# A hybrid encoder on one core: dense matmuls placed between transposes, score products and norm sums, with TensorE's order pinned to the source

## Chip, cores and metric

The kernel runs on one core of one Trainium2 chip. The metric is the device time of one execution in microseconds; lower is better. Five engines run side by side, each through its own list of instructions: TensorE (PE; its weight loads are shown apart as PEld), VectorE (DVE), ScalarE (ACT), GpSimd (POOL) and SyncE (SP, which issues DMAs). An engine whose next instruction waits for another engine stands still, and so does everything behind it in its list.

## What is computed

Two layers of an encoder over 512 tokens of 1024 features, in float32. Each layer mixes tokens in three ways from one projection of the normed input, merges the three by gates, and goes on with a gated feed-forward part and a small embedding part. Cut to what matters here:

```python
for i in range(DEPTH):                                   # DEPTH = 2
    h = rmsnorm(x, mix_norm[i])
    u_rnn, u_gelu, c_q, ckv_rope, fq, fk, fv, f_logit, gate_logit = split_columns(h @ w_in[i])
    y_a = rglru_branch(u_rnn, u_gelu, ...) @ w_br_a[i]   # gated recurrence
    y_b = mla_branch(c_q, ckv_rope, ...) @ w_br_b[i]     # latent attention, 8 heads
    y_c = fox_branch(fq, fk, fv, f_logit, ...) @ w_br_c[i]   # forgetting attention, 8 heads
    g = sigmoid(gate_logit + gate_b[i]).reshape(B, S, 3, D)
    x = x + (g[:, :, 0] * y_a + g[:, :, 1] * y_b + g[:, :, 2] * y_c) @ w_o[i]
    hf = rmsnorm(x, ffn_norm[i]) @ w_gate_up[i]
    x = x + (silu(hf[..., :D_FF]) * hf[..., D_FF:]) @ w_down[i]
    x = x + sigmoid(rmsnorm(x, ple_norm[i]) @ w_ple_gate[i]) * (p[i] @ w_ple[i])
return rmsnorm(x, final_norm)

# both attentions, per head and block of 128 queries (fox adds decay[t] - decay[s] to the logits)
s = where(mask, einsum('bqhd,bkhd->bhqk', q_blk, k) * scale, NEG_INF)
o = einsum('bhqk,bkhd->bqhd', softmax(s), v)
```

## The kernel before

**Products.** Every float32 operand is held as two float32r parts, hi and lo, whose sum is the value. A product of a 128x128 weight tile with 128 features of all 512 tokens is then three matmuls, hi by hi, hi by lo and lo by hi (`mm3`, L239), all into one PSUM bank. There are eight banks, of which the program's names `bank_67` to `bank_74` speak. `dense` (L246) is a generator for one output tile: it takes a bank, runs `mm3` once per k tile (8 for 1024 features), yields after each k tile, and hands the bank to its evacuation on VectorE or ScalarE. `group` and `values` are the same for several output tiles side by side; `values` makes the attention's values, token-major.

**Weights.** `Stream` keeps them flowing: SyncE loads units of four tiles, ScalarE casts the hi part (L112), VectorE subtracts to get the lo part (L113). A ring holds five split units. This work stands in the lists of ScalarE and VectorE among all the rest.

**Norms.** `norm_sum` sums squares over the partitions with four matmuls of one column (operand `one`), takes 1/sqrt with a dozen tiny VectorE instructions, and builds diagonals of it, hi and lo, with four instructions each. `norm_bcast` spreads them over all partitions with two matmuls (operand `onesr`). `after_norm` (L352) runs the first dense products behind a norm and puts sums and broadcast between their steps.

**Attention.** `attention(fox, odd, plan, tail)` is one loop over steps t, eight heads by four query tiles and three steps more. Step t does, in the source: the score products of tile t (two matmuls for fox, three for the latent attention, 128 to 512 columns wide); the products with the values of a head whose four tiles are done (`pv_mm`, eight matmuls); the transposes of tile t-2 (one to four, 128x128, L828, operand `identr`); on VectorE the mask addition (`fmask`, fox only, L221), the row maximum (L836) and, for tile t-1, the reciprocal and the scaling by it (L842, L225); on ScalarE the exponential (L230); and the copies of the transposed tile as `pth` (ScalarE, L853) and `ptl` (VectorE, L221). The values' products read `pth` and `ptl`. At the end of a step `fill` runs a share of the dense products that `plan` lists for this pair of heads: what is left, divided by the steps left, in k tiles. The plan holds merges, gates, branch projections, the projections of the next heads, and in fox's last pair the norm sums and broadcasts of the two latent norms.

**What sets the order.** Within the source's data dependences the framework's scheduler reorders each engine's instructions by a simulated timeline (`schedule_with_timeline_sim=True`). An instruction given to `tc.keep_in_program_order` keeps its place among others so given. Before, none of TensorE's instructions in attention is. Each engine then runs its list in order.

Of the kernel before, what the change touches and what calls it, by code (L numbers as in the profile page):

```python
# [17 lines left out]
DEPTH, SEQ, D = 2, 512, 1024  # L18
# [8 lines left out]
# columns of w_in  # L27
# [3 lines left out]
# columns of the small per-partition vectors, per layer  # L31
V_MIX, V_FFN, V_PLE, V_GB, V_CW, V_CB, V_BA, V_BX, V_QN, V_KN, V_BF = (
    0, 8, 16, 24, 48, 64, 68, 72, 76, 79, 81)
NV = 82
V_LAM = DEPTH * NV          # lambdas of all layers, side by side
# [3 lines left out]
NUNITS = 606                # units of four 128x128 weight tiles in the stream  # L39
KEPT = NUNITS - 16          # from here on the stream is kept on chip: it is used twice  # L40
PACKED = (8, 9, 311, 312)  # units whose tiles hold the parts of 64 columns side by side


class Pages:
    """Pages of one tile, handed out oldest-freed first."""
# [39 lines left out]
class Stream:  # L85
    """The weights, in the order in which TensorE uses them: loaded ahead, split into two
    float32r parts that sum to the float32 value."""
# [46 lines left out]
    def tile(self, spec):  # L134
        """hi and lo of the next 128x128 tile"""
# [7 lines left out]
    def again(self, i):  # L143
        """tile i of the stream, one of those that were kept"""
        return self._parts(i // 4, slice(128 * (i % 4), 128 * (i % 4) + 128))
# [6 lines left out]
    def wide(self, spec):  # L152
        """hi and lo of a 128x512 tile, at the start of a unit"""
# [13 lines left out]
class Trunk:  # L167
    def __init__(self, ctx, tc, wst, vec, xT, pT, trig, masks, outT, last):
# [32 lines left out]
        self.defer = None  # L201

    # -- small things ---------------------------------------------------------------------

    def cols(self, n):
        """n columns of a ring of small per-partition values"""
# [29 lines left out]
    def mm(self, out, a, b, start, stop):  # L236
        self.nc.tensor.matmul(out, a, b, start=start, stop=stop, skip_group_check=True)  # L237

    def mm3(self, out, ah, al, bh, bl, start, stop):  # L239
        self.mm(out, ah, bh, start, False)  # L240
        self.mm(out, ah, bl, False, False)
        self.mm(out, al, bh, False, stop)

    # -- products, as generators that stop after every k tile -----------------------------

    def dense(self, spec, xs, evac, m=128):  # L246
        """out[m, tokens] = sum over k of W[k, m] * X[k, tokens]; xs are pages"""
        b = self.banks.take()
        n = len(xs)
        for k, x in enumerate(xs):  # L250
            wh, wl = self.w.tile(spec + (k,))
            self.mm3(b[:m], wh[:, :m], wl[:, :m], x.h, x.l, k == 0, k == n - 1)
# [6 lines left out]
    def group(self, specs, xs, evacs):  # L259
        """several of them side by side, k tile by k tile"""  # L260
        bs = [self.banks.take() for _ in specs]
        n = len(xs)
        for k, x in enumerate(xs):
            for b, spec in zip(bs, specs):
                wh, wl = self.w.tile(spec + (k,))
                self.mm3(b[:, :], wh, wl, x.h, x.l, k == 0, k == n - 1)
# [1123 lines left out]
```

## Time and profile before

| what | value |
|---|---|
| runs of the kernel, median of 3 | 1825.26 us |
| lowest and highest | 1824.38, 1826.84 us |
| the profiled execution, from first to last instruction (its span) | 1825.0 us |
| mean granted clock of TensorE | 0.996 of full speed |
| ScalarE's casts of the weights (L112) | 590, 364.3 us busy |
| VectorE's subtractions for the weights (L113) | 590, 404.2 us busy |
| score and value products (L237 from `pr`) | 704, 120.7 us busy |

The profile gives no time of that execution beside its span; the span lies 0.26 us below the median of the runs. A row of a timeline reads: start, length, engine, line, operation, output and input by the program's names with buffer numbers left out, their shapes, and a count where like instructions follow each other. In brackets stands the idle time ahead of it with the instruction that ended it. An instruction's length includes its way through the engine's pipeline, so that the next one starts before it ends. A row of windows has the length of the stretch, each engine's busy time with its count of instructions, TensorE's granted clock, the busy share of the DMA engines and their GB/s.

### The profile page before, as it was taken

Reading aid. Unit: us, or ns where it says so; the run is one execution under the profiler, and the core shown is the slowest. Engines: PE = TensorE matmul, PEld = TensorE weight load, DVE = VectorE, ACT = ScalarE, POOL = GpSimd, SP = SyncE. Lnnn points to the kernel's source line nnn. Section 1 sums busy time; section 2 is a strip of 40 time slices with the busy share of each in tenths; the row PEclk is TensorE's granted clock in tenths of the full one; section 3 lists DMA queues with packets and bytes.
Section 4 is the critical chain, followed back from the end, with each engine's and each line's share of the span. In section 5 each row is a group of like instructions: output and inputs, shape, how many; then the busy total and the mean of one; then the engine's idle time right before and its main releaser. Section 6 shows DMA issues by size and latency. Waiting matters only on the chain. (4 is left out here: it accounts for less than half of the span.)

```text
span 1825.0 us, 24155 instructions
## 1 busy us (share of the span) xinstructions
PE 1807.5 (99%) x8490; PEld 1505.6 (82%) x8490; DVE 1210.6 (66%) x2421; ACT 817.1 (45%) x1562; POOL 117.2 (6%) x234
## 2 busy tenths in 40 slices
PE   9999999999999999999999999999999999999998
PEld 8778888888888888888887788888888888888887
DVE  8997678866665555444778966888576555553457
ACT  4766556553333333223447655565533333332243
POOL 1220001100000000000103200010000000000000
PEclk9999999999999999999999999999999999999999
DMA  5232223324222222322333322242232222232231
GB/s 178 91 131 82 81 78 117 97 72 139 96 95 96 96 98 98 110 94 97 133 110 122 106 81 82 91 116 85 87 128 92 99 98 97 95 109 99 98 116 47
DMA packets 98826, 184.17 MB, mean 101 GB/s; under 512 B 13552, under 2 KB 14752, under 8 KB 98704
## 3 DMA queue, kind: packets, MB, share of 16 engines
q1 hardware_dynamic: 89280, 162.04, 25.7%
q0 software_dynamic: 8416, 19.45, 3.8%
q8 instruction: 66, 1.08, 0.2%
q10 hardware_dynamic: 1008, 1.14, 0.2%
q14 instruction: 56, 0.46, 0.1%
HBM read 173.98 MB, written 4.21 MB: 98 GB/s over the span
## 5 line engine op out<-in xcount | busy, mean ns | idle before, releaser
L237 PE MATMUL bank<-pr,hl 128*128 128x512 f32 (+1 forms) x6812 | 1602.9, 392 | 2.8 <-ACT pr L233 1.1
L237 PEld LDWEIGHTS bank<-pr,hl 128*128 128x128 f32 (+1 forms) x6812 | 1269.9, 188 | 267.3 <-ACT pr L233 2.0
L112 ACT CAST hl<-raw 128x512 fp32r<-128x512 f32 x590 | 364.3, 618 | 672.0 <-PE bank L237 403.8
L113 DVE TENSOR_TENSOR hl<-raw,hl 128x512 fp32r<-128x512 f32 x590 | 404.2, 686 | 378.6 <-ACT hl L112 360.4
L221 DVE TENSOR_TENSOR pf<-pf 128x512 f32<-128x512 f32 (+3 forms) x235 | 151.1, 651 | 31.8 <-ACT pf L230 29.9
L221 DVE TENSOR_TENSOR pf<-bank,pf 128x512 f32<-128x512 f32 (+3 forms) x198 | 132.8, 676 | 58.6 <-PE bank L237 32.1
L230 ACT ACTIVATE pf<-pf 128x512 f32<-128x512 f32 (+1 forms) x145 | 86.1, 600 | 112.7 <-DVE pf L221 110.5
L237 PE MATMUL bank<-pr 128*128 128x256 f32 (+5 forms) x704 | 120.7, 303 | 4.1 <-ACT pf L230 2.2
L237 PEld LDWEIGHTS bank<-pr 128*128 128x128 f32 (+1 forms) x704 | 102.7, 191 | 14.1 <-ACT pf L230 2.7
L221 DVE TENSOR_TENSOR pr<-pf,pr 128x512 fp32r<-128x512 f32 (+2 forms) x126 | 85.6, 682 | 4.5 <-ACT pr L233 3.5
L230 ACT ACTIVATE pf<-bank,small 128x384 f32<-128x384 f32 (+3 forms) x130 | 68.9, 531 | 38.5 <-DVE small L836 35.4
L233 ACT CAST pr<-pf 128x512 fp32r<-128x512 f32 (+1 forms) x114 | 70.4, 620 | 33.2 <-DVE pf L218 23.1
L853 ACT CAST pth<-bank 128x128 fp32r<-128x128 f32 (+3 forms) x128 | 54.0, 427 | 58.7 <-PE bank L828 50.5
L221 DVE TENSOR_TENSOR ptl<-bank,pth 128x128 fp32r<-128x128 f32 (+3 forms) x128 | 61.7, 485 | 13.9 <-ACT pth L853 9.9
L836 DVE TENSOR_REDUCE small<-bank 128x1 f32<-128x384 f32 (+3 forms) x128 | 61.6, 484 | 7.6 <-PE bank L237 6.5
L237 PE MATMUL bank<-hl,pr 128*128 128x512 f32 x240 | 56.3, 391 | 0.4 <-DVE hl L113 0.4
L828 PE MATMUL bank<-identr,pf 128*128 128x128 f32 x320 | 55.0, 273 | 0.0
L237 PEld LDWEIGHTS bank<-hl,pr 128*128 128x128 f32 x240 | 44.7, 188 | 10.3 <-DVE hl L113 1.1
L225 DVE TENSOR_SCALAR pf<-pf,small 128x384 f32<-128x384 f32 (+3 forms) x128 | 48.6, 383 | 2.6
L828 PEld LDWEIGHTS bank<-identr,pf 128*128 128x128 f32 x320 | 40.2, 140 | 8.3
L218 DVE SCALAR_TENSOR_TENSOR pf<-pf,bank 128x512 f32<-128x512 f32 x48 | 32.6, 683 | 21.6 <-PE bank L237 21.2
L230 ACT ACTIVATE pf<-bank,vec 128x512 f32<-128x512 f32 x60 | 40.9, 689 | 12.9 <-PE bank L237 12.5
(112 smaller groups left out, 796.6 us busy)
## 6 DMA issues: line engine op xcount, KB each, us to landing
raw<-wst SPq DMA_DIRECT2D x606, 256.0 KB, 2.6
pf<-xT POOLq DMA_DIRECT2D x16, 256.0 KB, 3.3
pr<-pr POOLq DMA_DIRECT2D x32, 128.0 KB, 2.6
pf<-xs POOLq DMA_DIRECT2D x16, 256.0 KB, 3.2
pf<-trig POOLq DMA_DIRECT2D x12, 256.0 KB, 3.1
pf<-xT SPq DMA_DIRECT2D x8, 256.0 KB, 5.3
xs<-pf POOLq DMA_DIRECT2D x8, 256.0 KB, 2.7
pf<-pT POOLq DMA_DIRECT2D x4, 256.0 KB, 3.1
```

The costliest lines, as they stand in the source:

```text
L112: self.nc.scalar.copy(hi, src)
L113: self.nc.vector.tensor_tensor(lo, src, hi.bitcast(F32), op=ALU.subtract)
L218: self.nc.vector.scalar_tensor_tensor(out, a, s, b, op0=op0, op1=op1)
L221: self.nc.vector.tensor_tensor(out, a, b, op=op)
L225: self.nc.vector.tensor_scalar(out, a, s1, None, op0=op0)
L230: return self.nc.scalar.activation(out, a, f, **kw)
L233: self.nc.scalar.copy(hi, src)
L237: self.nc.tensor.matmul(out, a, b, start=start, stop=stop, skip_group_check=True)
L828: nc.tensor.transpose(T[:, c], p2.ap[:, c], self.ident[:, :])
L836: nc.vector.reduce_max(R[t][:, 0:1], S[:, :m], axis=AX.X, negate=True)
L853: self.nc.scalar.copy(hi, src)
```

## The change

`fill` now counts single matmuls, not k tiles. It puts one dense matmul ahead of every transpose and between the score products of a tile; what is left of a step's share comes at its end. `mm3` became a generator, `mm3s`, that yields between its three matmuls, and `dense`, `group` and `values` yield with it. While `attention` runs, `self.pinned` is set, and every matmul and transpose is given to `keep_in_program_order`, so that TensorE runs them as the source has them. `norm_sum` can run one matmul of the dense products between its four, and `after_norm` makes use of that. The tail of the last steps is 14 matmuls instead of 6 k tiles. Comments went too, and lines moved by a few: L237, L218, L221 and L225 are L238, L219, L222 and L226 after, the transposes L828 are L849, L836 and L842 are L857 and L863.

```diff
     def mm(self, out, a, b, start, stop):
-        self.nc.tensor.matmul(out, a, b, start=start, stop=stop, skip_group_check=True)
+        i = self.nc.tensor.matmul(out, a, b, start=start, stop=stop, skip_group_check=True)
+        if self.pinned:
+            self.tc.keep_in_program_order(i)
 
     def mm3(self, out, ah, al, bh, bl, start, stop):
+        self.run(self.mm3s(out, ah, al, bh, bl, start, stop))
+
+    def mm3s(self, out, ah, al, bh, bl, start, stop):
         self.mm(out, ah, bh, start, False)
+        yield
         self.mm(out, ah, bl, False, False)
+        yield
         self.mm(out, al, bh, False, stop)
...
     def dense(self, spec, xs, evac, m=128):
...
-            self.mm3(b[:m], wh[:, :m], wl[:, :m], x.h, x.l, k == 0, k == n - 1)
+            yield from self.mm3s(b[:m], wh[:, :m], wl[:, :m], x.h, x.l, k == 0, k == n - 1)
             yield
...
-    def norm_sum(self, st, n, fold=None):
+    def norm_sum(self, st, n, fold=None, between=None):
...
             self.mm(b[:, j:j + 1], acc.ap[:, j * 128:(j + 1) * 128], self.one[:, 0:1], True, True)
+            if between is not None:
+                between()
...
         for i, _ in enumerate(gen):
-            if i + 1 == s1:
-                self.norm_sum(st, n)
-            if i + 1 == s2:
+            if i + 1 == 3 * s1:
+                self.norm_sum(st, n, between=lambda: next(gen))
+            if i + 1 == 3 * s2 - st["n"] // 128:
                 self.norm_bcast(st)
...
-            def fill(m):
-                nonlocal left
+            def fill(m=1):
+                nonlocal left, spent
+                if t >= n and not todo:
+                    next(tail, None)
                 while m > 0 and todo:
                     try:
                         next(todo[0])
                         m -= 1
                         left -= 1
+                        spent += 1
                     except StopIteration:
                         todo.pop(0)
...
+            self.pinned = True
             for t in range(n + 3):
...
-                    left = sum(c for _, c in plan[t // 8])
+                    left = 3 * sum(c for _, c in plan[t // 8])
+                share, spent = -(-left // (8 - t % 8)), 0
...
                         self.mm(S[:, :m], q.h[:, c], k.h[:, :m], True, False)
+                        fill()
                         self.mm(S[:, :m], q.l[:68, c], k.l[:68, :m], False, True)
...
-                        nc.tensor.transpose(T[:, c], p2.ap[:, c], self.ident[:, :])
+                        fill()
+                        self.tc.keep_in_program_order(
+                            nc.tensor.transpose(T[:, c], p2.ap[:, c], self.ident[:, :]))
...
-                    fill(-(-left // (8 - t % 8)))
+                    fill(share - spent)
                 else:
                     drain()
-                    for _ in range(6):
+                    for _ in range(14):
                         next(tail, None)
...
+            self.pinned = False
```

The lists of instructions show what this moves. **TensorE, start of layer 0's fox attention**, right behind the last matmuls of the values. Before, where rows with `pr,hl` are dense matmuls and rows with `pr` alone are score products:

```order
L237 MATMUL bank_68<-pr,hl 128x512 x9
L237 MATMUL bank_73<-pr 128x128
L237 MATMUL bank_68<-pr,hl 128x512 x5
L237 MATMUL bank_69<-pr 128x256
L237 MATMUL bank_70<-pr,hl 128x512
L237 MATMUL bank_68<-pr,hl 128x512 x10
L237 MATMUL bank_70<-pr,hl 128x512 x5
L237 MATMUL bank_73<-pr 128x128
L237 MATMUL bank_69<-pr 128x256
```

The same place after the change. The piece begins with the second score product of tile 0; ahead of it, behind the values, stand only that tile's first product and one dense matmul:

```order
L238 MATMUL bank_73<-pr 128x128
L238 MATMUL bank_68<-pr,hl 128x512 x19
L238 MATMUL bank_69<-pr 128x256
L238 MATMUL bank_68<-pr,hl 128x512
L238 MATMUL bank_69<-pr 128x256
L238 MATMUL bank_68<-pr,hl 128x512 x3
L238 MATMUL bank_70<-pr,hl 128x512 x16
L238 MATMUL bank_71<-pr 128x384
L238 MATMUL bank_70<-pr,hl 128x512
L238 MATMUL bank_71<-pr 128x384
L238 MATMUL bank_70<-pr,hl 128x512
L849 MATMUL bank_74<-identr,pf 128x128
```

The second score product stood 30 dense matmuls behind the values and stands one behind them now; the first transpose (L828, now L849) stood 126 dense matmuls behind the values and stands 42 behind them now. In layer 1 it is 132 before and 42 after.

**VectorE in the same stage.** Its list is the same before and after up to the fourth evacuation of the values and one scalar_tensor_tensor (`pf<-pf,vec`) behind it. From there before has 35 instructions up to and with the scaling of tile 0, the last row of this piece:

```order
L113 TENSOR_TENSOR hl<-raw,hl 128x512
L221 TENSOR_TENSOR pr<-pf,pr 128x512
L842 RECIPROCAL small<-small 128x1
L836 TENSOR_REDUCE small<-bank_68 128x1
L221 TENSOR_TENSOR pr<-pf,pr 128x512
L221 TENSOR_TENSOR bank_73<-bank_73,fmask 128x128
L225 TENSOR_SCALAR pf<-pf,small 128x128
```

After the change there are 23, the last of which are:

```order
L857 TENSOR_REDUCE small<-bank_69 128x1
L222 TENSOR_TENSOR pr<-pf,pr 64x512
L219 SCALAR_TENSOR_TENSOR pf<-pf,vec 128x512
L222 TENSOR_TENSOR pr<-pf,pr 64x512
L219 SCALAR_TENSOR_TENSOR pf<-pf,vec 128x512
L863 RECIPROCAL small<-small 128x1
L857 TENSOR_REDUCE small<-bank_71 128x1
L863 RECIPROCAL small<-small 128x1
L222 TENSOR_TENSOR pr<-pf,pr 128x512
L226 TENSOR_SCALAR pf<-pf,small 128x128
```

The scaling of tile 0 moved forward by twelve instructions. In layer 1 there are 43 instructions of VectorE from the low part of head 0's queries to that scaling.

**TensorE from the latent norms' sums to their broadcasts**, in fox's last pair of heads, layer 0. The sums are the rows with `one`, the broadcasts those with `onesr`. Before:

```order
L237 MATMUL bank_69<-one,pf 128x1 x4
L237 MATMUL bank_70<-pr,hl 128x512 x18
L237 MATMUL bank_68<-pr 128x256 x2
L828 MATMUL bank_74<-identr,pf 128x128 x4
L237 MATMUL bank_70<-pr,hl 128x512 x6
L237 MATMUL bank_72<-pr,hl 128x512 x7
L237 MATMUL bank_67<-pr,onesr 128x512
L237 MATMUL bank_72<-pr,hl 128x512 x5
L237 MATMUL bank_73<-pr 128x384 x2
L237 MATMUL bank_72<-pr,hl 128x512
L237 MATMUL bank_69<-pth,pr 128x512
L237 MATMUL bank_67<-pr,onesr 128x512
```

After, from the second of the two score products behind the sums (fifteen dense matmuls, a score product and one dense matmul stand between the sums and this piece):

```order
L238 MATMUL bank_70<-pr 128x256
L238 MATMUL bank_69<-pr,hl 128x512
L849 MATMUL bank_68<-identr,pf 128x128
L238 MATMUL bank_69<-pr,hl 128x512
L849 MATMUL bank_68<-identr,pf 128x128
L238 MATMUL bank_69<-pr,hl 128x512
L849 MATMUL bank_68<-identr,pf 128x128
L238 MATMUL bank_69<-pr,hl 128x512
L849 MATMUL bank_68<-identr,pf 128x128
L238 MATMUL bank_69<-pr,hl 128x512 x4
L238 MATMUL bank_67<-pr,onesr 128x512 x2
L238 MATMUL bank_73<-pr,onesr 128x512 x2
```

The four transposes stand one by one between dense matmuls, and the four broadcasts follow each other behind 24 dense matmuls, where before they lay scattered behind 31 and more. In the latent attention six dense matmuls (three for the first head) and three score products of 384 columns now stand between the four transposes of a head's last tile and its products with the values. Of the norms outside attention, the sums are separated in the two embedding norms; elsewhere they stay in a row, since the scheduler orders them.

More of the change, by code (lines that the diff above doesn't have):

```diff
@@ L265, in group @@
                 wh, wl = self.w.tile(spec + (k,))
-                self.mm3(b[:, :], wh, wl, x.h, x.l, k == 0, k == n - 1)
+                yield from self.mm3s(b[:, :], wh, wl, x.h, x.l, k == 0, k == n - 1)
                 yield
@@ L613, in values @@
                     c = slice(j * 128, (j + 1) * 128)
-                    self.mm3(bs[j][:, :], x.h[:, c], x.l[:, c], wh, wl, k == 0, k == len(X) - 1)
+                    yield from self.mm3s(bs[j][:, :], x.h[:, c], x.l[:, c], wh, wl, k == 0, k == len(X) - 1)
                     yield
@@ L754, in attention @@
             z2, pv = [], []
-            todo, left = [], 0
-            def fill(m):
-                nonlocal left
+            todo, left, spent = [], 0, 0
+            def fill(m=1):
+                nonlocal left, spent
+                if t >= n and not todo:
+                    next(tail, None)
                 while m > 0 and todo:
@@ L813, in attention @@
                         self.mm(S[:, :m], q.h[:100, c], k.h[:100, :m], True, False)
+                        fill()
                         self.mm(S[:, :m], q.h[:96, c], k.l[:96, :m], False, False)
+                        fill()
                         self.mm(S[:, :m], q.l[:96, c], k.h[:96, :m], False, True)
@@ L827, in attention @@
                         c = slice(128 * j, 128 * j + 128)
-                        nc.tensor.transpose(T[:, c], p2.ap[:, c], self.ident[:, :])
+                        fill()
+                        self.tc.keep_in_program_order(
+                            nc.tensor.transpose(T[:, c], p2.ap[:, c], self.ident[:, :]))
                     p2.free()
@@ L866, in attention @@
                 pv_out(hp, pv_mm(hp))
+            self.pinned = False
             for p in self.V:
@@ L1152, in part @@
                     wh, wl = self.w.again(4 * KEPT + KD * j + k)
-                self.mm3(b[:, :SEQ // 2], wh, wl, X[k].h[:, t], X[k].l[:, t], k == 0, k == KD - 1)
+                yield from self.mm3s(b[:, :SEQ // 2], wh, wl, X[k].h[:, t], X[k].l[:, t], k == 0, k == KD - 1)
                 yield
```

## Prediction

> **What bounds the kernel now.** I read the page first, its busy times and costliest groups, to see which engine sets the end:
>
> ```profile
> span 1825.0 us, 24155 instructions
> PE 1807.5 (99%) x8490; PEld 1505.6 (82%) x8490; DVE 1210.6 (66%) x2421; ACT 817.1 (45%) x1562; POOL 117.2 (6%) x234
> L237 PE MATMUL bank<-pr,hl 128*128 128x512 f32 (+1 forms) x6812 | 1602.9, 392 | 2.8 <-ACT pr L233 1.1
> L828 PE MATMUL bank<-identr,pf 128*128 128x128 f32 x320 | 55.0, 273 | 0.0
> ```
>
> TensorE is busy in 1807.5 of 1825.0 us, so it stands idle for 17.5 us, the start of the program included. Nothing that only fills its idle time can win more than that. The other way to gain is to make its steps cheaper. The transposes have no idle time ahead of them at all. So two questions decide: does a transpose cost less between two dense matmuls than in a run, and what does TensorE wait for once its order is fixed by the source instead of by the scheduler? The list of TensorE's waits shows where its idle time lies now:
>
> ```profile
> PE bank L237 <- ACT pf L230: 2.2, 1, 2.2
> PE bank L237 <- DVE pf L218: 1.3, 1, 1.3
> ```
>
> The 1.3 us stand in layer 0 and the 2.2 us in layer 1, both where the forgetting attention (fox) begins. That is the stage to look at.
>
> **Part 1: what a transpose costs.** An instruction's duration includes its way through the array, so I count from start to start. In the timeline of TensorE, in layer 0's fox attention:
>
> ```profile
> 135.22 0.27 PE L828 MATMUL bank<-identr,pf 128*128 128x128 f32 x1
> 135.24 0.48 PE L237 MATMUL bank<-pr,hl 128*128 128x512 f32 x1
> 135.56 0.71 PE L828 MATMUL bank<-identr,pf 128*128 128x128 f32 x5
> 136.02 1.41 PE L237 MATMUL bank<-pr,hl 128*128 128x512 f32 x5
> 137.27 0.81 PE L828 MATMUL bank<-identr,pf 128*128 128x128 f32 x6
> 137.84 2.99 PE L237 MATMUL bank<-pr,hl 128*128 128x512 f32 x12
> ...
> 143.87 6.08 PE L237 MATMUL bank<-pr,hl 128*128 128x512 f32 x26
> 149.78 0.34 PE L237 MATMUL bank<-pr 128*128 128x128 f32 x2
> ```
>
> Twenty-six dense matmuls take 149.78 - 143.87 = 5.91 us, 0.227 each. A lone transpose with its dense matmul takes 135.56 - 135.22 = 0.34 us: 0.227 and **0.113** for the transpose. Five transposes and five dense matmuls take 137.27 - 135.56 = 1.71 us; less 5 x 0.227 that is 0.575, or **0.115** for each transpose. The step right behind the lone one looks cheap (0.02 us), but the dense matmul after it then takes 0.32. So a transpose costs the same in both places. I take separation at nothing for the transposes, and from the few hundredths that such readings scatter by, about 0.003 us on 320 of them and as much on the score products, I put 1.2 us on it, with bounds of -3 and +3.
>
> By the Trainium skill, "TensorE: Matmul & The Clock Gate", "Back-to-back issue gap", 128-column matmuls follow each other at about 81 ns in a stream that loads weights, and at about 56 ns alone. If a neighbour hid that difference of 25 ns, some 200 transposes that now follow another would bring 5 us, and the sum would be 5 us lower; the lone one's 0.113 us against 0.115 in the run shows no such saving.
>
> **Part 2: the fox attention starts at once.** Before, the scheduler put dense work ahead of what was not ready. The fixed order puts score tiles 0, 1 and 2 and then the first transpose behind only 42 dense matmuls. That transpose needs the softmax of tile 0, which VectorE ends. In layer 0:
>
> ```profile
> 97.79 2.20 PE L237 MATMUL bank<-pr,hl 128*128 128x512 f32 x9
> ...
> 104.88 0.47 PE L237 MATMUL bank<-pr 68*128 68x128 f32 x2
> ...
> 122.85 0.50 PE L237 MATMUL bank<-pr,hl 128*128 128x512 f32 x1 [0.40 <-ACT pr L233]
> 124.65 0.80 PE L237 MATMUL bank<-pr 128*128 128x256 f32 x2 [1.30 <-DVE pf L218]
> 125.97 9.41 PE L237 MATMUL bank<-pr,hl 128*128 128x512 f32 x29 [0.53 <-DVE pf L221]
> ```
>
> The values end at 97.79. From there to the first transpose at 135.22 before has 126 dense matmuls (28.6 us) and twelve score products, about 1.8 us (3,328 columns are 1.5 us at the dense rate, and the short ones cost more than their columns). That is 30.4 of 37.43 us, so before loses 7.0 us there: part in waits and part in what follows them (below).
>
> After the change, two waits come. The first is for the low parts of head 0's queries, which a VectorE instruction in the row of three at 103.50 makes. In before the product started at 104.88; now it is the third TensorE instruction after the values, and one dense matmul stands ahead of it, so TensorE waits some 6.7 us. The second is at the first transpose. VectorE's order is the same as before up to 111.84; I price what follows by its rows:
>
> ```profile
> 103.50 2.00 DVE L221 TENSOR_TENSOR pr<-pf,pr 128x512 fp32r<-128x512 f32 x3
> 111.84 0.68 DVE L113 TENSOR_TENSOR hl<-raw,hl 128x512 fp32r<-128x512 f32 x1
> 112.45 0.74 DVE L218 SCALAR_TENSOR_TENSOR pf<-pf,vec 128x512 f32<-128x512 f32 x1
> 113.11 0.68 DVE L221 TENSOR_TENSOR pr<-pf,pr 128x512 fp32r<-128x512 f32 x1
> 115.51 0.49 DVE L221 TENSOR_TENSOR bank<-bank,fmask 128x128 f32<-128x128 f32 x2
> ...
> 128.10 0.54 DVE L225 TENSOR_SCALAR pf<-pf,small 128x128 f32<-128x128 f32 x2
> ```
>
> Between the row at 111.84 and the scaled tile 0, VectorE now has 23 instructions: 14 of 512 columns (0.61 from start to start, 0.66 for the scalar form: together 8.8) and nine short ones (0.07 to 0.47, the mask addition 0.20 to 0.25: together 2.0). So tile 0 is ready at 111.84 + 10.8 = **122.6**, where before had it at 128.3. The first transpose, were nothing waited for, would start at 97.79 + 42 x 0.227 + 0.82 for six score products = 108.2. TensorE loses 14.4 us to both waits.
>
> What follows a wait costs too. The table of windows over layer 0 shows it:
>
> ```profile
> core 0: us, PE busy (x) PEld busy (x) DVE busy (x) ACT busy (x) POOL busy (x), PEclk, DMA share, GB/s
> ...
> 126.00:131.00 5.00, 5.00 (x12) 3.94 (x13) 4.75 (x14) 1.65 (x4) 0.00 (x0) 0.50 0.36 109
> ```
>
> After the three short waits of before the granted clock was 0.50 for 5 us, in which only 12 matmuls ran: 12 x 0.227 = 2.7, so 2.3 us were lost. After a wait of 7.7 us I count the same 2.3. The first wait may slow the clock too, but that only shortens the second wait, as tile 0's time is VectorE's. Layer 0: 14.4 + 2.3 - 7.0 = **+9.7 us**.
>
> The Trainium skill, "TensorE: Matmul & The Clock Gate", "Why this matters for your kernels", asks for no TensorE gap above about 3 us, since half clock follows for a window of 3.4 us. That speaks against this change, and the window's 0.50 agrees; by its window a stall costs 1.7 us, and the sum over both layers would be 1.2 us lower.
>
> Layer 1, the same place:
>
> ```profile
> 998.45 0.22 PE L237 MATMUL bank<-pr 128*128 128x128 f32 x1
> ...
> 1002.05 0.30 PE L237 MATMUL bank<-pr 68*128 68x128 f32 x1 [0.58 <-issue]
> ...
> 1034.96 1.25 PE L828 MATMUL bank<-identr,pf 128*128 128x128 f32 x10
> ```
> ```profile
> 1001.28 1.39 DVE L221 TENSOR_TENSOR pr<-pf,pr 64x512 fp32r<-64x512 f32 x2
> ```
> ```profile
> 1001.30:1024.80 23.50, 20.05 (x89) 15.89 (x89) 23.34 (x42) 17.12 (x32) 7.28 (x15) 1.00 0.40 133
> ```
>
> Before runs 132 dense matmuls (30.0) and 1.8 us of scores in 36.51 us, so it loses 4.7. Now VectorE has 43 instructions from 1001.28 to the scaled tile 0. The window shows that it does 42 of the like in 23.5 us and rests for 0.2: tile 0 is ready at 1024.8. Without waits the transpose would start at 998.45 + 9.54 + 0.82 = 1008.8. That is 16.0 us lost, and 2.3 by the clock, less 4.7: **+13.6 us**. VectorE is the engine that is waited for in both; nothing hides this, as TensorE may not pass the waiting instruction. ScalarE's exponential lies between VectorE's steps with room (17.12 of the 23.5 us busy).
>
> **Part 3: the broadcasts of the latent norms.** Their four products are now pinned behind the norm sums, with 24 dense matmuls, two score products and four transposes ahead of them: 24 x 0.227 + 0.24 + 4 x 0.113 = 6.1 us. Before had:
>
> ```profile
> 254.50 1.84 PE L237 MATMUL bank<-one,pf 128*128 128x1 f32 x16
> ...
> 269.57 0.40 PE L237 MATMUL bank<-pr,onesr 128*128 128x512 f32 x1
> ```
> ```profile
> 264.71 0.34 DVE L218 SCALAR_TENSOR_TENSOR pr<-identr,small,pr 128x128 fp32r<-128x128 f32 x1
> ```
>
> The sums end at 256.3, and the last piece of their diagonals ends at 265.05, 8.75 us later; the scheduler put the last broadcast at 269.57. Six to seven us is not enough: a wait of 2.0 to 2.6 us per layer, **+4.6 us** for two. If VectorE takes the diagonals together, 0; if a dense result comes in between, twice that.
>
> **Part 4: the latent attention's products with the values.** Six dense matmuls and three score products of a later head now stand between a head's fourth transpose tile and the first product: about 2.45 us. Before took 390.18 - 384.72 = 5.5:
>
> ```profile
> 384.72 0.60 PE L828 MATMUL bank<-identr,pf 128*128 128x128 f32 x4
> 386.03 0.69 DVE L221 TENSOR_TENSOR ptl<-bank,pth 128x512 fp32r<-128x512 f32 x1
> 390.18 0.39 PE L237 MATMUL bank<-pth,pr 128*128 128x512 f32 x1
> ```
>
> Here the copies end 386.72 - 384.72 = 2.0 us after the first transpose, in time by 0.45. One wide VectorE instruction ahead of them (0.6) makes it late by 0.15, two by 0.75. I take 0.15 us a head on the 16 latent heads: **+2.4 us**, bounds 0 and 16 x 0.75 = 12. Fox heads have 3.9 us there and wait for nothing.
>
> **Sum.** 1.2 + 9.7 + 13.6 + 4.6 + 2.4 = 31.5 us. The profiled execution took 1825.0; the median of the runs is 1825.26, which the sum is added to: **1856.8 us**.
>
> **The rivals.** *Separation works.* A transpose between dense matmuls costs only the 0.02 to 0.03 us of its own step, since its weight load hides: 200 that now stand in runs would win 200 x 0.09 = 18 us, and the 17.5 us of idle time bound what else can go. With no stalls added: 1825.3 - 18 - 10 = 1797. The rows at 135.22 to 137.27 speak against it, and the waits of part 2 would have to be absent. *Only the starts wait, and the clock holds.* The broadcasts and the values' products find VectorE ahead after the stall and the clock recovers within the wait: 14.4 + 16.0 - 7.0 - 4.7 = 18.7, so 1844. For it: at most places VectorE has room (66% busy). *Pinned value products wait at most heads.* VectorE takes dense results ahead of the copies; 12 us in part 4 instead of 2.4 and 9 in part 3 instead of 4.6: 1871. Against it: the copies come soon in 384.72 to 386.72. *Nothing moves*, because the scheduler already chose a like order: 1825. The lists of instructions exclude it: runs of transposes are gone.
>
> **How the numbers follow.** Forecast 0.55, only the starts 0.22, value products wait 0.16, separation works 0.05, nothing moves 0.02. Its own unknowns move the forecast by -8 to +10. The range reaches from below the second case to above the third: 1838 to 1876. A measurement of this kernel can tell about 0.2% (3.7 us) from no change: faster 0.04, within 0.03, slower 0.93.
>
> **What would show it.** In the changed profile: TensorE's longest waits are at the second score product (near 98 us) and at the first transpose (released by VectorE's scaling, near 122.6 and 1024.8), with a clock near 0.5 behind them; a transpose and a dense matmul in turn take 0.34 us together; broadcasts wait 2 us. It would be wrong if the pair took 0.26 us, or if tile 0 were scaled near 110 us.

## The result, and the profile after

The changed kernel takes **1858.33 us** (median of 4 runs, 1857.85 to 1858.43), beside 1825.49 for the kernel before in the same session: a ratio of 1.0179, with a 95% interval of 1.0165 to 1.0194. It is slower, and lies 1.5 us above the forecast of 1856.8. The span of the profiled execution is 1856.6 us against 1825.0. (An execution's time lies 1.7 to 3.0 us above its span in the runs for which both are on record, so the span of 1825.0 belongs to an execution near the highest of the three, 1826.84 us: the spans differ by 31.6 us, the medians by 32.8.) Its page, the busy times and the groups of the transposes and of the score and value products:

```profile
span 1856.6 us, 24139 instructions
PE 1813.2 (98%) x8490; PEld 1504.3 (81%) x8490; DVE 1218.8 (66%) x2421; ACT 814.4 (44%) x1562; POOL 116.1 (6%) x234
L238 PE MATMUL bank<-pr 128*128 128x256 f32 (+4 forms) x704 | 148.6, 297 | 9.6 <-issue 8.6
L849 PE MATMUL bank<-identr,pf 128*128 128x128 f32 x320 | 87.0, 272 | 18.2 <-DVE pf L226 18.2
```

The transposes show 87.0 us of busy time where they showed 55.0. That isn't their cost: transposes in an unbroken run overlap and the overlap is counted once, so a run looks cheap and single ones dear. What changed is the last column. Transposes that had no idle time ahead of them now have 18.2 us, ended by VectorE's scaling of the probabilities (L226). The list of TensorE's waits says how few places that is:

```profile
PE bank L849 <- DVE pf L226: 18.2, 2, 12.7
PE bank L238 <- issue: 8.6, 2, 5.2
PE bank L238 <- DVE pr L219: 2.4, 2, 1.2
PE bank L238 <- DVE pr L226: 1.6, 2, 0.8
...
PE bank L238 <- DVE ptl L222: 0.8, 2, 0.4
```

Each of these five is met twice, once per layer: at the first transpose, at the second score product, at the broadcasts of the latent norms, and at one head's value products. The two waits at the start of fox attention, in the timeline of TensorE, layer 0 first, then layer 1:

```profile
98.00 0.33 PE L238 MATMUL bank<-pr 128*128 128x128 f32 x1 [1.07 <-ACT pr L575]
98.17 0.44 PE L238 MATMUL bank<-pr,hl 128*128 128x512 f32 x1
103.85 0.45 PE L238 MATMUL bank<-pr 68*128 68x128 f32 x1 [5.24 <-issue]
104.09 6.75 PE L238 MATMUL bank<-pr,hl 128*128 128x512 f32 x19
...
121.94 0.47 PE L849 MATMUL bank<-identr,pf 128*128 128x128 f32 x1 [5.49 <-DVE pf L226]
122.07 6.13 PE L238 MATMUL bank<-pr,hl 128*128 128x512 f32 x18
...
1014.77 0.30 PE L238 MATMUL bank<-pr 68*128 68x128 f32 x1 [3.31 <-issue]
...
1037.74 0.47 PE L849 MATMUL bank<-identr,pf 128*128 128x128 f32 x1 [12.69 <-DVE pf L226]
```

"issue" names no releaser, but the product of 103.85 is the one that reads the low parts of head 0's queries. In layer 0 the first score product waits as well, 1.07 us for ScalarE, which the prediction did not have. VectorE hardly pauses there: it is busy for 5.97 us of the window from 98 to 104 us, and for 5.87 of that from 116 to 122. Two rows of its timeline bound the backlog, the last evacuation of the values and the scaling of tiles 0 and 1:

```profile
109.49 0.75 DVE L219 SCALAR_TENSOR_TENSOR pr<-bank,small,pr 128x512 fp32r<-128x512 f32 x1
...
121.61 0.54 DVE L226 TENSOR_SCALAR pf<-pf,small 128x128 f32<-128x128 f32 x2
```

To see where 31.6 us of span came from, I cut both executions at four places that TensorE passes in both after about the same work: the end of the values in each layer (start of the last value matmul and 0.23 us), and the first sum of the latent norms in each layer. The stages in us:

| stage | before | after | difference | predicted |
|---|---|---|---|---|
| start to end of values, layer 0 | 97.79 | 96.77 | -1.0 | 0 |
| fox start, to the latent norms' sums, layer 0 | 156.70 | 166.40 | +9.7 | +9.7 |
| from there to the end of values, layer 1 | 743.96 | 747.78 | +3.8 | +3.5 |
| fox start, to the latent norms' sums, layer 1 | 154.43 | 167.54 | +13.1 | +13.6 |
| the rest | 672.15 | 678.13 | +6.0 | +3.5 |

(Of the prediction's terms, half of broadcasts and value products stands in the third and fifth row each; the 1.2 us of alternation stand in none.) The first stage's 1.0 us is no part of the change: in the fourteen profiled executions of this study it takes 96.4 to 98.0 us.

### The profile page after: what moved, and what is told of

Same layout as the page of the kernel before. It is cut to its first block, busy times and chain, and to the rows that moved or that the text cites. A ratio compares the mean times of both kernels' runs of the same rounds, so it can differ in the third digit from the quotient of the medians.

```text
span 1856.6 us, 24139 instructions
## 1 busy us (share of the span) xinstructions
PE 1813.2 (98%) x8490; PEld 1504.3 (81%) x8490; DVE 1218.8 (66%) x2421; ACT 814.4 (44%) x1562; POOL 116.1 (6%) x234
## 3 DMA queue, kind: packets, MB, share of 16 engines
q1 hardware_dynamic: 89280, 162.04, 26.4%
## 4 chain that ended last, share of the span: by engine, by line
PE 95%; DVE 2%; issue 1%; ACT 0%; POOL 0%; DVEq 0%; POOLq 0%
PE bank L238 93%; PE bank L849 2%; DVE pf L219 1%; DVE pr L222 1%; DVE hl L113 0%; DVE pf L222 0%; POOL pf L389 0%; POOL pf L390 0%; ACT pr L575 0%; ACT pr L234 0%; DVE pr L219 0%; DVE ptl L222 0%; DVE pf L226 0%; POOL pf L387 0%; DVE pr L226 0%
## 5 line engine op out<-in xcount | busy, mean ns | idle before, releaser
L238 PE MATMUL bank<-pr,hl 128*128 128x512 f32 (+1 forms) x6812 | 1647.9, 396 | 0.7 <-ACT pr L234 0.7
L238 PEld LDWEIGHTS bank<-pr,hl 128*128 128x128 f32 (+1 forms) x6812 | 1273.4, 189 | 277.2 <-ACT pr L234 1.2
L222 DVE TENSOR_TENSOR pf<-bank,pf 128x512 f32<-128x512 f32 (+3 forms) x198 | 132.9, 676 | 64.1 <-PE bank L238 43.2
L222 DVE TENSOR_TENSOR pf<-pf 128x512 f32<-128x512 f32 (+3 forms) x235 | 151.4, 652 | 31.6 <-ACT pf L231 29.6
L238 PE MATMUL bank<-pr 128*128 128x256 f32 (+4 forms) x704 | 148.6, 297 | 9.6 <-issue 8.6
L238 PEld LDWEIGHTS bank<-pr 128*128 128x128 f32 (+1 forms) x704 | 108.1, 191 | 18.1 <-issue 9.1
L849 PE MATMUL bank<-identr,pf 128*128 128x128 f32 x320 | 87.0, 272 | 18.2 <-DVE pf L226 18.2
L231 ACT ACTIVATE pf<-bank,small 128x512 f32<-128x512 f32 (+3 forms) x130 | 68.8, 530 | 59.5 <-DVE small L857 54.6
L222 DVE TENSOR_TENSOR pr<-pf,pr 128x512 fp32r<-128x512 f32 (+2 forms) x126 | 85.3, 683 | 2.6 <-ACT pr L234 2.1
L857 DVE TENSOR_REDUCE small<-bank 128x1 f32<-128x128 f32 (+3 forms) x128 | 62.5, 488 | 18.5 <-PE bank L238 16.6
L222 DVE TENSOR_TENSOR ptl<-bank,pth 128x128 fp32r<-128x128 f32 (+3 forms) x128 | 62.1, 485 | 13.4 <-ACT pth L874 12.4
L849 PEld LDWEIGHTS bank<-identr,pf 128*128 128x128 f32 x320 | 45.2, 141 | 20.6 <-DVE pf L226 18.9
L238 PE MATMUL bank<-hl,pr 128*128 128x512 f32 x240 | 56.2, 390 | 0.0
L238 PEld LDWEIGHTS bank<-hl,pr 128*128 128x128 f32 x240 | 44.9, 188 | 9.7 <-DVE hl L113 0.4
L226 DVE TENSOR_SCALAR pf<-pf,small 128x128 f32<-128x128 f32 (+3 forms) x128 | 49.4, 387 | 3.2
L219 DVE SCALAR_TENSOR_TENSOR pf<-pf,bank 128x512 f32<-128x512 f32 x48 | 32.7, 684 | 23.9 <-PE bank L238 22.6
```

The lines of the kernel that those rows point to most:

```text
L219: self.nc.vector.scalar_tensor_tensor(out, a, s, b, op0=op0, op1=op1)
L222: self.nc.vector.tensor_tensor(out, a, b, op=op)
L226: self.nc.vector.tensor_scalar(out, a, s1, None, op0=op0)
L231: return self.nc.scalar.activation(out, a, f, **kw)
L238: i = self.nc.tensor.matmul(out, a, b, start=start, stop=stop, skip_group_check=True)
L849: nc.tensor.transpose(T[:, c], p2.ap[:, c], self.ident[:, :]))
```

## Experiments

The same cut for every kernel that ran: stages 1 to 5 as above, in us of the profiled execution, and the median of its runs beside the ratio to the kernel before on the same chip with its 95% interval.

| kernel | 1 | 2 | 3 | 4 | 5 | median | ratio |
|---|---|---|---|---|---|---|---|
| before | 97.79 | 156.70 | 743.96 | 154.43 | 672.15 | 1824.76 to 1825.49, by session | |
| after | 96.77 | 166.40 | 747.78 | 167.54 | 678.13 | 1858.33 | 1.0179 (1.0165 to 1.0194) |
| 1 nothing pinned | 96.42 | 157.80 | 743.54 | 160.41 | 672.39 | 1832.82 | 1.0040 (1.0025 to 1.0055) |
| 2 pinned, unbroken runs | 97.25 | 167.03 | 745.57 | 168.36 | 673.96 | 1854.23 | 1.0157 (1.0141 to 1.0172) |
| 3 pinned from step 8 | 97.84 | 158.23 | 749.32 | 159.47 | 678.08 | 1844.17 | 1.0102 (1.0087 to 1.0117) |
| 4 same, broadcasts free | 96.88 | 157.72 | 749.42 | 159.13 | 677.86 | 1842.79 | 1.0095 (1.0078 to 1.0112) |
| 5 as 4, unbroken runs | 97.79 | 158.61 | 745.47 | 159.42 | 673.96 | 1836.44 | 1.0058 (1.0041 to 1.0075) |
| 6 waits filled | 97.29 | 166.09 | 747.72 | 166.13 | 678.17 | 1857.05 | 1.0170 (1.0155 to 1.0186) |
| 7 before, renorm late | 96.99 | 151.52 | 743.86 | 155.31 | 672.43 | 1821.86 | 0.9980 (0.9971 to 0.9990) |
| 8 after, renorm late | 97.76 | 160.29 | 747.76 | 163.09 | 676.63 | 1847.20 | 1.0118 (1.0103 to 1.0133) |
| 9 share only | 96.86 | 157.68 | 743.88 | 160.41 | 672.39 | 1833.28 | 1.0048 (1.0034 to 1.0061) |
| 10 sums earlier | 97.37 | 163.46 | 748.80 | 165.41 | 678.01 | 1854.28 | 1.0159 (1.0145 to 1.0175) |
| 11 before, renorm spread | 97.79 | 154.28 | 743.26 | 155.22 | 672.27 | 1824.80 | 0.9999 (0.9991 to 1.0008) |
| 12 before, renorm mid | 97.97 | 152.78 | 743.23 | 152.52 | 672.17 | 1820.26 | 0.9973 (0.9963 to 0.9983) |

(In kernel 10 the sums stand earlier by 12 dense matmuls and, with them, three transposes and two score products of 128 columns: 12 x 0.227 us and five at some 0.12 us, together 3.3 us. Its stages 2 and 4 are shorter by that, 3 and 5 longer.)

**Pins, alternation, counting: 1, 2 and 9.** Kernel 1 is the change without its pins:

```diff
-            self.pinned = True
...
-                        self.tc.keep_in_program_order(
-                            nc.tensor.transpose(T[:, c], p2.ap[:, c], self.ident[:, :]))
+                        nc.tensor.transpose(T[:, c], p2.ap[:, c], self.ident[:, :])
```

> The changed kernel with the dense matmuls written between transposes and score products, but nothing pinned. Theory (the fixed order makes TensorE wait, separation itself is worth nothing): the waits at the first transposes go, and the time is 1825 to 1830 us, 28 to 33 us below the changed kernel. Rival (the alternation itself costs TensorE time): 1845 us or more. Rival (separation gains and pinning hides it): below 1821 us.

Kernel 2 is the change without its alternation; kernel 9 has both edits, so that only the counting in single matmuls and the tail of 14 matmuls a step are left. (The expectation below calls that tail longer; in matmuls it is shorter, as 6 k tiles are 18. It lies at the end of each attention, not at the starts.) The first line goes at all its four places:

```diff
-                        fill()
...
-                self.norm_sum(st, n, between=lambda: next(gen))
+                self.norm_sum(st, n)
-            if i + 1 == 3 * s2 - st["n"] // 128:
+            if i + 1 == 3 * s2:
```

> The changed kernel with its pins, but with the dense matmuls back at the end of each step, so that transposes, score products and norm sums run unbroken. Theory: the first transposes wait as long as in the changed kernel (at about 122 us and 1038 us of the span), so 1855 to 1858 us; the alternation's own cost, 1 to 3 us, is all that goes. Rival (alternation costs): 1825 to 1832 us. Rival (alternation gains): above 1863 us.

> Nothing pinned and nothing alternated: of the change only the counting of a step's share in single matmuls (20 at first, where it was 7 k tiles, 21 matmuls) is left, and the longer tail. The kernel with alternation and no pins was 7.7 us slower than before, 6 of them at the starts of the two fox attentions. Theory now (the scheduler's list at those starts shifts with the share, whatever alternates): 1829 to 1833 us, with TensorE waits at the start of layer 1's fox attention. Rival (the alternation in the source made it): 1824 to 1826 us.

With the change itself these make a square. Free and unbroken 1833.28, free and alternating 1832.82, pinned and unbroken 1854.23, pinned and alternating 1858.33. (They ran in three sessions, in which the kernel before took 1824.76, 1825.12 and 1825.49.) **The pins cost 20.9 us with unbroken runs and 25.5 with alternation. Alternation costs nothing measurable when the order is free and 4.1 us, waits and clock included, when it is pinned.** With the order free the scheduler undoes part of the alternation: the busy time of the transposes is 71.4 us in kernel 1, between 54.5 in kernel 9 and 87.0 in the change. And 8.5 us stand in neither: counting in matmuls, with nothing pinned, is already slower than before. Kernel 1 missed its expectation by 3 us for that reason. All four kernels of the square share that count; none pins the old one. Kernel 2, just below its range, keeps the waits of the change without any alternation:

```profile
103.07 0.44 PE L238 MATMUL bank<-pr 68*128 68x128 f32 x1 [4.92 <-DVE pr L222]
...
123.03 0.48 PE L845 MATMUL bank<-identr,pf 128*128 128x128 f32 x1 [8.39 <-DVE pf L226]
```

Here the trace names the releaser of the second score product, VectorE's subtraction into `pr`. In kernel 9's timeline TensorE's waits stand at the same stage, of layer 1 here, but elsewhere in it:

```profile
1016.36 0.44 PE L238 MATMUL bank<-pr 128*128 128x128 f32 x2 [1.11 <-DVE pf L222]
1021.78 11.86 PE L238 MATMUL bank<-pr,hl 128*128 128x512 f32 x40 [4.98 <-DVE pf L222]
```

A step's share of 20 matmuls instead of 21 gave the scheduler another list, in which TensorE waits 4.98 us for one of VectorE's products into `pf`, where the longest wait of the kernel before was 2.2. In the table this shows in stage 4: 160.41 against 154.43. Why the scheduler's simulated timeline chose that list was not tried.

**The starts freed: 3, 4 and 5.** Kernel 3 pins only from step 8 on:

```diff
-            self.pinned = True
             for t in range(n + 3):
+                self.pinned = not fox or t >= 8
...
```

(The transposes are pinned by the same condition.)

> The changed kernel, but pinned only from the third head on in each layer's fox attention (from step 8). Theory: the 9.7 and 13.1 us lost at the two starts go and all else stays: 1835.5 us, between 1832 and 1839. Rival (the fixed order costs all through attention): above 1845 us.

It takes 1844.17 us, far above its range and just below the rival's 1845. Stages 2 and 4 fell by 8.2 and 8.1 us, not by the 9.7 and 13.1 that would bring them back to the kernel before: 158.23 and 159.47 are near kernel 9's 157.68 and 160.41, so what stays looks like the counting's. The miss has a second part, 1.5 us in stage 3: behind the same broadcast waits as in the change, half clock now follows in layer 0 too (a granted clock of 0.63 from 267 to 271 us, where the change had 1.00).

Kernel 4 also leaves the four broadcasts free, and kernel 5 takes kernel 4's alternation away by kernel 2's edit:

```diff
+                self.pinned = False
                 self.norm_bcast(s)
+                self.pinned = True
```

> As the kernel pinned only from step 8, and the four broadcasts of the latent norms not pinned either. Theory: their waits of 2.5 us a layer and the half clock that follows in layer 1 go too, 5 to 6.6 us less: 1829 to 1831 us. Rival (what waits is VectorE's lateness, and TensorE meets it at the next instruction): no less than the kernel pinned from step 8, about 1835 us.

> Pinned from step 8 and broadcasts free, as the kernel before it, but with the dense matmuls at the end of each step, so that transposes and score products run unbroken. With few waits left, this prices the alternation. Theory (a transpose costs 0.11 us either way, and single ones some 0.01 more): 1 to 3 us less than the kernel with alternation, about 1828 us. Rival (a dense matmul hides the transpose's weight load): 5 to 18 us more.

Kernel 4 takes 1842.79 us, 12 us above its range, and tells nothing of its question: free to move, the broadcasts stayed behind the same 24 dense matmuls, and still waited. Its timeline:

```profile
264.03 0.50 PE L238 MATMUL bank<-pr,onesr 128*128 128x512 f32 x1 [0.81 <-DVE pr L226]
265.74 0.60 PE L238 MATMUL bank<-pr,onesr 128*128 128x512 f32 x1 [1.21 <-DVE pr L219]
```

Kernel 5 is 6.4 us below kernel 4, twice what was expected. In the profiled executions stages 3 and 5, where the latent attentions lie, are 3.9 us shorter each. In the fox stages 2 and 4 alternation costs nothing that can be seen (157.72 and 158.61, 159.13 and 159.42). Not all of the 3.9 us is the alternation's own. One head of the latent attention, from its predecessor's first value product to its own, has the same 78 matmuls and no wait in both, kernel 4 first:

```profile
331.57:346.98 15.41, 15.41 (x79) 12.72 (x79) 13.05 (x30) 9.47 (x22) 2.55 (x5) 1.00 0.24 78
```
```profile
330.12:345.32 15.20, 15.20 (x79) 12.84 (x79) 12.58 (x30) 9.87 (x22) 1.54 (x3) 1.00 0.25 79
```

(Each row also counts the matmul that runs into its window.) Alternation makes the head 0.21 us longer, an estimated 1.7 us for eight. The rest is waits and clock: kernel 4 loses about 1.5 us to half clock behind its broadcasts (0.51 from 266.0 to 269.5 us), 0.3 us more to the broadcast waits, and 0.4 us to a wait at one head's value products; in kernel 5 the broadcasts wait once, for 1.73 us, and the clock stays at 1.00.

**The broadcasts: 10.** Instead of freeing them, kernel 10 gives them more to stand behind:

```diff
-            lkv + [mg(0, 7, yA), (free_yA(), 0), (latent_sums(), 0), gt(2, 0), (latent_norm(), 0),
+            lkv + [(gate(0, 7, box7), 8), (latent_sums(), 0), (branch(0, 7, yA, box7), 4), (free_yA(), 0),
+                   gt(2, 0), (latent_norm(), 0),
```

> The changed kernel with the latent norms' sums 12 dense matmuls (2.7 us) earlier, ahead of the last branch product instead of behind it, so that 36 dense matmuls stand ahead of the broadcasts instead of 24. Theory (the pinned broadcasts wait for the diagonals by 2.5 us a layer, and half clock follows once): the waits go, 5 to 6.6 us less, 1852 to 1853 us. Rival (VectorE comes later too, so the wait moves on): 1857 to 1858 us.

The four follow each other without a wait, in the timeline of kernel 10 and, for comparison, of the change:

```profile
272.14 1.07 PE L238 MATMUL bank<-pr,onesr 128*128 128x512 f32 x4
```
```profile
271.19 0.61 PE L238 MATMUL bank<-pr,onesr 128*128 128x512 f32 x2
272.61 0.50 PE L238 MATMUL bank<-pr,onesr 128*128 128x512 f32 x1 [0.81 <-DVE pr L226]
274.32 0.50 PE L238 MATMUL bank<-pr,onesr 128*128 128x512 f32 x1 [1.21 <-DVE pr L219]
```

The time fell by 4.05 us where 5 to 6.6 were expected. Corrected for the 3.3 us, stages 3 and 5 are 2.3 and 3.4 us shorter, together the 5.7 us of the theory: distance cures the waits, and the half clock behind them in layer 1 is gone. Stages 2 and 4 are 0.4 and 1.2 us longer. In layer 1 half clock lasts longer behind the first transpose: the 18 dense matmuls there take 6.8 us up to the next score product, where the change needs 5.5. Why it lasts longer was not tried.

**The clock: 6.** Matmuls without use, on operands that are ready, fill the waits:

```diff
+            def busy(m):
+                b = self.banks.tiles[0]
+                for _ in range(m):
+                    self.mm(b[:, :], qp[0].h[:, 0:128], kp[0].h[:, :], True, True)
...
+                        if t == 0:
+                            busy((20, 12)[L])
...
+                        if fox and t == 2:
+                            busy((20, 48)[L])
```

> The changed kernel with added matmuls of no use in its two waits of each layer (20 and 20 in layer 0, 12 and 48 in layer 1, each 512 wide), so that TensorE isn't idle there. The first transposes still start when VectorE has scaled tile 0, near 122 and 1038 us. Theory (half clock behind an idle TensorE costs 1.7 and 1.4 us behind the first transposes, and what it costs ahead of them is hidden in the wait): 3.1 us less, 1855 us. Rival (the clock costs nothing or can't be kept): 1858 us; rival (clock also costs ahead of the transposes): 1853 us or less.

It fell by 1.3 us, less than half of what was expected. In layer 1 the added matmuls left 1.79 us of wait ahead of the first transpose, and the clock held; the same window in the change and in kernel 6:

```profile
1037.70:1041.20 3.50, 3.46 (x10) 2.79 (x11) 1.43 (x5) 0.89 (x2) 0.00 (x0) 0.58 0.00 0
```
```profile
1037.70:1041.20 3.50, 3.45 (x16) 2.88 (x17) 2.26 (x6) 1.61 (x3) 0.00 (x0) 1.00 0.00 0
```

Sixteen matmuls instead of ten, at a clock of 1.00 instead of 0.58; stage 4 is 1.4 us shorter. In layer 0 twenty were too few: 3.14 us of wait were left, and the clock behind it was low again:

```profile
122.36 0.33 PE L858 MATMUL bank<-identr,pf 128*128 128x128 f32 x1 [3.14 <-DVE pf L226]
```
```profile
122.00:127.00 5.00, 4.64 (x14) 3.72 (x15) 3.04 (x9) 2.19 (x5) 0.00 (x0) 0.66 0.03 11
```

The Trainium skill, "TensorE: Matmul & The Clock Gate", "Why this matters for your kernels", puts the limit at a gap of about 3 us. A wait of 1.79 us that left the clock whole and one of 3.14 that was followed by half clock lie on either side of it, so these two agree. The broadcasts don't: behind waits of 0.81 and 1.21 us, neither near 3 us, half clock came in some runs too (last section).

**VectorE's list as the cause: 7, 8, 11 and 12.** In fox's first pair VectorE makes a normed copy of the input, two instructions of 512 columns for each of eight pages, part of them while TensorE waits for tile 0. Kernels 7 (on the kernel before) and 8 (on the change) move that to the end of the pair:

```diff
-            [fp(1, 0, X, st["r"]), (renorm(0, 1), 0), mg(0, 0, yA, X, st["r"]), (renorm(2, 3, 4), 0),
-             mg(0, 1, yA, X, st["r"]), (renorm(5, 6, 7), 0), (drop_x(), 0), fp(1, 1), mg(0, 2, yA)],
+            [fp(1, 0, X, st["r"]), mg(0, 0, yA, X, st["r"]), mg(0, 1, yA, X, st["r"]),
+             fp(1, 1, X, st["r"]), (renorm(0, 1, 2), 0), mg(0, 2, yA, X, st["r"]),
+             (renorm(3, 4, 5, 6, 7), 0), (drop_x(), 0)],
```

> The kernel before, with VectorE's sixteen instructions of the renormed input (a product and a subtraction for each of eight pages) moved from the middle of the first pair of fox heads to its end; the products there use the un-normed input and scale their results, which adds some VectorE products. Theory (VectorE's backlog at the fox starts is what TensorE waits for, 11.8 us in both layers): 3 to 9 us less, 1816 to 1822 us. Rival (the backlog only moves to the end of the pair): 1823 to 1828 us, with waits there.

> The changed kernel with the same move of the renormed input. Theory (the first transpose waits for VectorE's list, which now has 3 to 5 us less ahead of tile 0's scaling): the first transposes start 2 to 5 us earlier in each layer, 1849 to 1854 us. Rival (something else is waited for there): 1858 us.

With the order still pinned the first transposes start 18.7 and 21.1 us behind the end of the values instead of 25.2 and 26.8, and the kernel is 11.1 us faster, more than expected. VectorE starts 33 and 38 instructions in that time instead of 44 and 48. Of the 11.1 us, 1.5 stand in stage 5: the broadcasts wait as before, but no half clock follows them in layer 1 (1.00 from 1180 to 1184 us), which the move did not aim at. TensorE's timeline in kernel 8, where the values end at 97.76 and 1005.81:

```profile
116.49 0.47 PE L849 MATMUL bank<-identr,pf 128*128 128x128 f32 x1 [6.42 <-DVE pf L226]
```
```profile
1026.93 0.47 PE L849 MATMUL bank<-identr,pf 128*128 128x128 f32 x1 [6.29 <-DVE pf L226]
```

So it is VectorE's list that sets those starts: a shorter one brings them forward, and the releaser stays the same. On the kernel before the same move brings 0.20% and leaves two waits for the copies of transposed tiles at the end of the pair, 2.4 us by the list of waits. Kernels 11 and 12 look for a middle, with the pages made two at a time through the pair, and two, three and three in its second half; their diffs, in this order:

```diff
+            [fp(1, 0, X, st["r"]), mg(0, 0, yA, X, st["r"]), (renorm(0, 1), 0), mg(0, 1, yA, X, st["r"]),
+             (renorm(2, 3), 0), fp(1, 1, X, st["r"]), (renorm(4, 5), 0), mg(0, 2, yA, X, st["r"]),
+             (renorm(6, 7), 0), (drop_x(), 0)],
```
```diff
+            [fp(1, 0, X, st["r"]), mg(0, 0, yA, X, st["r"]), mg(0, 1, yA, X, st["r"]), (renorm(0, 1), 0),
+             fp(1, 1, X, st["r"]), (renorm(2, 3, 4), 0), mg(0, 2, yA, X, st["r"]),
+             (renorm(5, 6, 7), 0), (drop_x(), 0)],
```

> The kernel before with the renormed input made two pages at a time between the products of the first fox pair, all of which use the un-normed input; each pair of pages comes later than before, none as late as in the kernel that moved most to the end. Theory (VectorE's backlog at the start costs TensorE 11.8 us before; moved to the end it left waits of 2.4 us there for the copies of transposed tiles): both get smaller, 1817 to 1821 us. Rival (any renorm at the start costs as before): 1823 to 1826 us.

> As the kernel with the renormed input spread, but two pages after the second merge product, three after the next projection and three at the end of the pair. Theory: between the kernel that moves it all late (1822 us) and the spread one, 1818 to 1822 us. Rival: 1823 to 1826 us.

The spread one is the same as before, against expectation, though its one profiled execution is 2.2 us shorter than that of the kernel before, which was one of its longer ones. **Kernel 12 takes 1820.26 us, 0.9973 of the kernel before, and is the fastest of all**, by 1.6 us from kernel 7, whose interval overlaps its own. Its gain stands in the two fox starts (152.78 and 152.52 against 156.70 and 154.43). The window from 88 to 130 us, in the kernel before and in kernel 12:

```profile
88.00:130.00 42.00, 39.37 (x163) 30.82 (x162) 41.75 (x78) 26.05 (x48) 14.10 (x28) 0.94 0.45 146
```
```profile
88.00:130.00 42.00, 40.99 (x188) 33.36 (x188) 41.75 (x83) 27.51 (x55) 9.71 (x19) 1.00 0.47 155
```

VectorE is busy for 41.75 of 42 us in both. What it does first has changed, and TensorE runs 188 matmuls where it ran 163, with 1.0 us of idle time instead of 2.6 and a clock of 1.00 instead of 0.94.

## Why the prediction was right

**What a transpose costs.** Right. In the changed kernel's timeline a transpose and a dense matmul in turn take 0.34 us, as the one lone transpose of before had shown:

```profile
133.99 0.27 PE L849 MATMUL bank<-identr,pf 128*128 128x128 f32 x1
...
134.33 0.27 PE L849 MATMUL bank<-identr,pf 128*128 128x128 f32 x1
...
134.67 0.27 PE L849 MATMUL bank<-identr,pf 128*128 128x128 f32 x1
```

So the rival in which separation works, which needed 0.26 us for the pair, is out. The term of 1.2 us for alternation was too small, and does not follow from its own counts (0.003 us on 320 transposes and as much again is 1.9). The rows of kernels 4 and 5 give 0.21 us for each latent head at full clock, an estimated 3.4 us for sixteen.

**The fox starts.** Right in place, releaser and size. Tile 0's transpose was put 24.8 and 26.4 us behind the end of the values; it came 25.2 and 26.8 us behind (121.94 - 96.77 and 1037.74 - 1010.95). In layer 1 the two waits are 3.31 + 12.69 = 16.0 us, as forecast. In layer 0 the waits are 1.07 + 5.24 + 5.49 = 11.8 us where 14.4 were forecast. Most of the rest went to the clock behind the first wait, at which 19 dense matmuls took 6.6 us instead of 4.3; that shortened the second wait, as the prediction had said. Two sizes partly cancelled. The first transposes came 0.4 us later in each layer than forecast, and the clock behind them, taken at 2.3 us a layer, cost less: behind the first transpose of layer 0 the trace has

```profile
122.00:127.00 5.00, 5.00 (x15) 4.01 (x16) 2.66 (x7) 1.61 (x3) 0.00 (x0) 0.62 0.01 3
```

fourteen dense matmuls and a transpose, 3.3 us of work in 5.0: 1.7 lost; by the window of kernel 6's comparison it is 1.4 in layer 1. The limit of 3 us for one gap, which the prediction set beside the clock of 0.50 in the kernel before, is not what that row shows: the waits ahead of it were 0.40, 1.30 and 0.53 us. The cause was put wholly on the fixed order. Stages 2 and 4 grew by 22.8 us, and kernel 9 has 7.0 of growth there (157.68 + 160.41 against 156.70 + 154.43) with nothing pinned, so unpinning alone does not win the 22.8 us back. How much the pins would cost with the old count is not shown. The number held because it was read from the changed kernel's own lists, which have the new count in them.

**Broadcasts.** Right: 0.81 + 1.21 = 2.0 us of wait in each layer, by the rows shown above, where 2.0 to 2.6 were forecast. Not forecast was half clock behind them in layer 1 alone:

```profile
1189.70:1194.00 4.30, 4.30 (x13) 3.44 (x14) 4.30 (x8) 2.86 (x5) 0.00 (x0) 0.63 0.18 59
```

**Latent value products.** Mis-sized: forecast at 0.15 us for each of 16 heads, they wait at one head in each layer, 0.41 us (0.8 in both by the list of waits). The middle and last stages lost 9.8 us where 7.0 were forecast. The runs account for it: 2.0 of broadcast waits, 0.4 here and an estimated 1.7 of alternation in each, and 1.4 of half clock in the last, 9.6 in all.

**The total.** Its closeness is in part luck: the value products and the clock at the fox starts were put too high by some 1.6 and 1.5 us, the alternation too low by some 2.2, and the 1.4 us of half clock behind the broadcasts of layer 1 was not forecast at all. These errors nearly cancel.

The rival without clock and later waits (1844) fell by the clock of 0.62 and by stages 3 and 5. The rival in which value products wait at most heads (1871) fell by that one wait of 0.41 us in a layer.

## What to carry to other kernels

Before an order is pinned, ask at each stage's start when the last engine in the chain delivers, counted from its own list: here a fixed order turned VectorE's backlog into waits of TensorE, where the free one had filled most of the gap with dense matmuls. Alternating long and short matmuls bought nothing where the lone one cost as much as one in a run; look for one lone specimen in the trace before the order is rebuilt. And where a scheduler sets the order, a change of a count that looks neutral can cost as much as the idea, so measure it alone.

## Not expected of the hardware

After waits of 0.81 and 1.21 us around one single matmul the granted clock of the change fell to 0.63 in layer 1 but not in layer 0, where the window behind the same two waits (274.3 to 278.0 us) shows 1.00. Five of the kernels have these same two waits in both layers, and half clock follows at six of the ten places: in layer 1 alone in the change and in kernel 6, in both layers of kernels 3 and 4, in neither of kernel 8. Layer 0 of kernel 4 first, then layer 1 of kernel 8:

```profile
266.00:269.50 3.50, 3.50 (x10) 2.69 (x10) 3.50 (x7) 3.04 (x6) 0.00 (x0) 0.51 0.13 47
```
```profile
1180.00:1184.00 4.00, 3.96 (x18) 3.31 (x19) 4.00 (x7) 3.31 (x7) 0.00 (x0) 1.00 0.17 62
```

So two microseconds of idle time in two pieces may or may not halve the clock. It cost 1.4 us in the change and 1.5 us in kernel 4's layer 0, enough to blur differences of that size between two kernels. Which moment decides was not tried.
